# A new hand-written order for the mixer of an encoder layer, with the first step of the second feed-forward layer in it

## The chip, the cores and the metric

The kernel runs on one core of a Trainium2 chip. The metric is the device time of one execution in microseconds (us); lower is better. A core has five engines that each run their own instructions strictly in order and wait for one another through semaphores: PE (TensorE, the matrix products), DVE (VectorE), ACT (ScalarE), POOL (GpSimd) and SP (here only a queue that issues DMAs). The time before is the median of three runs; the profile comes from one more execution.

## The reference, cut to what matters

One encoder layer on 512 positions of width 1024, all in float32: a feed-forward half step, a mixer, a second feed-forward half step and a last norm.

```python
def swiglu(h, w_gate, w_up, w_down):
    return (jax.nn.silu(h @ w_gate) * (h @ w_up)) @ w_down

def reference(x, ...):
    x = x + 0.5 * swiglu(rms_norm(x, ffn1_norm), ffn1_w_gate, ffn1_w_up, ffn1_w_down)
    h = rms_norm(x, mix_norm)
    u = h @ w_in                      # fourier group 512 | q 8x64 | k 2x64 | v 2x64
    f_out = fourier_mixer(u[..., :o0], fnet_w, fnet_b)       # Re(DFT2) per group, then a linear map
    a_out = gqa_attention(u[..., o0:o1], u[..., o1:o2], u[..., o2:], q_norm, k_norm)
    x = x + jnp.concatenate([f_out, a_out], axis=-1) @ w_out
    x = x + 0.5 * swiglu(rms_norm(x, ffn2_norm), ffn2_w_gate, ffn2_w_up, ffn2_w_down)
    return rms_norm(x, final_norm)
```

The feed-forward width is 2752. The attention has 8 query heads of 64 over 2 key heads, with a norm and an axial rotation on q and k.

## The kernel before, in words

The activations lie transposed, as eight tiles of 128 channels x 512 positions (`x[0]` to `x[7]`). Every float32 operand of a product is split into two parts, a rounded high part and the rest, so one product is three matmuls (`product`, L172 to L174): high x high, high x low, low x high. A weight block of 128 x 1024 is loaded by a DMA of the SP queue into one of three raw buffers, its high part is a copy (L865, or L164 in the feed-forward layers) on ACT or DVE, and its low part is raw minus high (`lows`, L131) on DVE or POOL. The splits go into pairs of slots of one ring, and a pair comes free when the last product with the old weights in it has been issued.

The kernel runs in three stages: the first feed-forward layer (0 to 336 us of the profile), the mixer (336 to 492 us) and the second feed-forward layer (492 us to the end). This text is about the mixer and the beginning of the stage behind it.

In the mixer each engine's order is not found by a scheduler. The work is cut into some 620 named operations (`op(...)`), and the string `ORDER` lists their names; the loop `for name in ORDER.split(): ops.pop(name)()` runs inside a block that fixes the order of all five engines as written. The names:

- `wk.r wk.h wk.l`: load of a weight block, its high part, its low part; likewise for `wq0` to `wq3`, `wv`, `f0` to `f3`, `fw`, and `o0` to `o7` of the output projection.
- `q2.5`: the sixth of the eight products of that projection (three matmuls on PE). `q2.sw`, `q2.sd`, `q2.rc`, `q2.rs`: rotation; `.sw` is on ACT, `.sd` are four small DMAs of the SP queue, `.rs` on DVE needs them. `.al` and `.bl` are low parts of the rotated q on DVE.
- `s102 m102 e102 x102 h102 l102`: one attention tile, 128 queries of one head against all 512 keys: scores (two matmuls on PE), scale and row minimum (DVE, L1227), exponential (ACT), 32 x 32 transposes (DVE, L1245), high part (ACT, or DVE if named in `HI_DVE`), low part (DVE, or POOL if named in `LOWS_POOL`). There are 32 tiles; the middle digit is the key head.
- `p0` to `p3`: 128 small matmuls each, probabilities x values of eight tiles. `o00.c o00.a` and so on take the result out (ACT, DVE), `z0.*` and `r0.*` scale it and split it.
- `f..`, `map.`, `d..`, `c..`: the Fourier branch.
- `y5.0` to `y5.7`: the eight products of output block 5; then `y5.x` adds them to `x[5]` (DVE, L1328), `y5.h` and `y5.l` are the two parts of the scaled input of the next layer (ACT, L199; DVE, L203), `y5.q` the square (ACT), `y5.a` its sum over blocks (`acc`, DVE, L1341).

PSUM has eight banks in the mixer (`mix0` to `mix7`), handed out in the order of the string: a product can also wait for the last reader of the bank that it is given.

The second layer opens with the gate block `gate(0, ...)` and the up block `gate(1, ...)`, eight products each. `gate` loads and splits its own weights, then walks k from 0 to 7; the dictionary `between` puts work ahead of a given k. Before the change, `column` (four small matmuls L231 that sum `acc` over the channels; DVE L238 and POOL L245 then make the inverse root) stands ahead of the last product of gate block 0, and `row` (four transposes, L250) ahead of product 3 of gate block 1:

```python
ffn(n2, n3, ..., GROUPS2, lambda gate, column, row: [[gate(0, {KD - 1: column}), gate(1, {3: row})]], Ending)
```

There PE and SP keep the order as written, and a scheduler places the work of DVE, ACT and POOL.

Of the kernel before, what the change touches and what calls it, by code (L numbers as in the profile page):

```python
# [56 lines left out]
k.sw q0.1 k.rc q0.2 q0.3 wq1.l n1.p wv.l q0.4 k.s0 k.s1 q0.5 f2.r q0.6 q0.7 q0.rc q1.0 k.s2 q0.sw q1.1 v.0 kw q1.2
q0.sq kp k.rs q1.3 q0.rs wq2.r q0.ah km k0.0 v.1 k0.2 wq2.h wq2.l q1.4 q1.5 q1.6 q1.7 q1.sw q0.bh v.2 v.3 q0.al k0.3
q0.pq v.4 wq3.r q2.0 q0.bl k1.0 v.5 k1.1 q1.sd v.6 q0.s0 q1.sq v.7 k0.1 q2.1 wq3.h q0.s1 q1.rc vt q1.pq q1.rs k1.3
s002 s003 q1.s0 q0.s2 f0.r f0.h s000 vp m003 wq3.l vm q2.2 m000 e003 q2.3 s001 x003 m002 f0.l m001 f1.r q1.s1 q2.4  # L60
q1.ah q2.5 q3.0 q2.6 q2.7 v0.h q1.al q1.bh h003 q3.1 e002 v0.l e000 x000 q2.sw q2.sq s103 q1.bl vr0.1 q3.2 s100 q3.3
f1.h q3.4 v1.h q3.5 q2.rc q1.s2 s102 s101 m103 x002 q3.6 l003 vr0.2 e103 m100 f1.l v1.l h000 q3.7 q2.sd q2.pq e001
e100 vr0.3 f00.0 q3.sw q2.rs f01.0 q3.sq m101 q3.pq x001 q2.s0 m102 l000 x100 h002 q2.s1 e101 q2.ah q2.al s200 f03.0
q3.sd x101 f3.r k1.2 f02.0 h001 q3.s0 q3.rc s202 q3.rs l002 f00.1 o5.r h100 f2.h q2.s2 q3.ah f3.h vr0.0 s203 q3.al
f2.l f02.1 q3.s1 x103 m203 e102 m202 l001 h101 s300 f00.u q2.bh e203 s201 f01.1 h103 x102 l101 f01.u q3.s2 h102 l103
l100 s302 f3.l f03.1 m200 m300 e202 q3.bh m302 f03.e f11.0 f02.e x203 l102 e302 f11.1 f02.h e200 x202 f03.h q3.bl
m201 fw.r f02.l fw.h e300 x200 p0 f11.u x300 s011 q2.bl e201 o2.r o00.c s303 s301 h203 h202 fw.l o01.c m011 z0.r
f10.0 pos o00.a m303 h200 o01.a h300 f10.1 m301 s012 s112 l203 l202 x201 e303 l200 o1.r s113 s110 h201 x303 m113
e301 f12.0 m112 f13.0 e113 l300 l201 x302 f03.l h303 e112 h302 m012 map1 l303 x301 f10.u f13.1 z1.r x112 map1.h
f12.1 map1.l h301 o2.h f13.e x113 e012 e011 l302 f13.h map0 f12.e f12.h m110 x012 map0.h o1.h l301 p1 f13.l f12.l  # L70
e110 s013 d00 o10.c d01 o11.c map0.l o2.l o1.l h112 x110 m013 vr1.1 d10 d01.h o10.a d00.h o11.a d01.l h012 d00.l d11
vr1.0 d10.h z0.w l112 s213 e013 d10.l x011 c0.s c0.q m213 h113 s111 s010 m010 d11.h h011 h110 s313 c0.c e010 d21
l012 d20 d11.l m111 m313 c1.c l113 e313 d21.h c0.o c1.s x013 d20.h x010 d31 c0.h c1.q d21.l s312 d20.l c0.l d30 s212
h010 l110 e111 z0.p l011 c1.o x111 c2.s o4.r h013 d30.h c1.h vr1.3 z1.w e213 y2.0 d31.h vr1.2 x313 l013 h111 s311
o0.r c2.q c1.l m312 d30.l l111 r0.m o0.h m212 c2.c e312 z1.p y2.1 d31.l e212 c3.c c3.s c2.o c3.q r1.m x212 c2.h c3.o
l010 r0.h m311 o0.l s310 m310 x312 e311 p2 c3.h c2.l e310 h212 c3.l r0.l y1.0 s211 o3.r x213 l212 h313 h312 m211
l313 z2.r s210 h213 l213 x311 m210 e211 o20.c y1.1 h311 y2.2 l312 y1.2 x211 e210 y1.3 o20.a h211 l311 o21.c x210
y2.3 y0.0 x310 y2.4 h210 z2.w h310 o21.a r1.h l210 l310 r1.l y0.1 y0.2 l211 z2.p z3.r y0.3 z3.w r2.m p3 r2.h y2.5
r2.l o30.c o30.a o31.c y2.6 y1.4 z3.p y1.5 y0.4 y1.6 o31.a r3.m r3.h r3.l y0.5 y2.7 o3.h y0.6 o3.l y1.7 y0.7 y3.0
o4.h o5.h y3.1 y3.2 y3.3 y3.4 o6.r o4.l o5.l y0.x y2.x y2.q y2.h y3.5 y4.0 y4.1 y4.2 y3.6 y3.7 y4.3 y4.4 y4.5 y5.0  # L80
# [1558 lines left out]
```

## Time and profile before

| | us |
|---|---|
| median of three runs | 839.28 (839.19 to 839.60) |
| the profiled execution | 835.62 |
| its span, first to last instruction | 833.8 |
| of it PE busy | 820.3 |
| DVE busy | 600.1 |
| ACT busy | 458.2 |
| POOL busy | 134.2 |

The profiled execution is 3.66 us (0.44%) shorter than the median of the runs. Sums below are made against 835.62, and their difference is then carried over to 839.28.

PE is busy nearly all the time, so what counts is its idle time: 13.5 us in the whole span, of which 6.6 us lie between 335 and 500 us. A row of the timeline gives the start, the duration, the engine, the line, the operation, what is written and what is read, and in brackets how long the engine had been idle and who ended that. Instructions overlap a little at their ends, so the distance from one start to the next is shorter than the duration: 0.60 against 0.68 for an `acc` sum, 1.13 against 1.22 for a weight split.

### The profile page before, as it was taken

What the parts mean: (1) busy time and instruction counts of PE and PEld (TensorE: products, weight loads), DVE (VectorE), ACT (ScalarE), POOL (GpSimd) and SP (SyncE); (2) the same over time, 40 slices, a digit from 0 to 9 for tenths busy, and PEclk for the clock granted to TensorE, in tenths of its full rate; (3) what the DMA queues carried; (4) which work ended last, traced back from release to release, by engine and by line L of the source; (5) the groups of instructions that cost most, each with busy time, mean ns of one, the idle gap of its engine ahead of it and who ended that gap; (6) DMA issues with size and microseconds to landing.
All of it is one profiled execution on the core that took longest, in us unless ns stands there. A gap on an engine that the chain in (4) does not pass through costs nothing.

```text
span 833.8 us, 14442 instructions
## 1 busy us (share of the span) xinstructions
PE 820.3 (98%) x5734; PEld 742.3 (89%) x5734; DVE 600.1 (72%) x938; ACT 458.2 (55%) x793; POOL 134.2 (16%) x140
## 2 busy tenths in 40 slices
PE   9999999999999999999989989999999999999997
PEld 6888998899989998889878878899988998899986
DVE  6987884578656857689998478878755884578562
ACT  7754663266434645477887348546533663366452
POOL 0121000000000000168795300200000000000001
PEclk9999999999999999999999999999999999999999
DMA  7787774467374413335351335877563774566122
GB/s 253 189 189 203 190 197 139 121 164 216 91 187 136 137 53 118 127 89 131 106 101 28 100 91 138 212 166 183 172 189 89 180 206 129 122 170 184 45 80 102
DMA packets 50725, 119.33 MB, mean 143 GB/s; under 512 B 5729, under 2 KB 14561, under 8 KB 50529
## 3 DMA queue, kind: packets, MB, share of 16 engines
q1 hardware_dynamic: 38128, 92.57, 33.7%
q0 software_dynamic: 12256, 25.57, 18.6%
q8 instruction: 45, 0.74, 0.4%
q10 hardware_dynamic: 272, 0.26, 0.1%
q14 instruction: 24, 0.19, 0.1%
HBM read 111.83 MB, written 2.10 MB: 137 GB/s over the span
## 4 chain that ended last, share of the span: by engine, by line
PE 89%; DVE 6%; ACT 2%; issue 1%; DMA 1%; POOL 0%; SPq 0%; POOLq 0%; DVEq 0%; ACTq 0%
PE r L441 23%; PE q L441 11%; PE dn L174 9%; PE dn L173 9%; PE dn L172 9%; PE p L441 6%; PE mix L172 3%; PE gu L172 2%; PE gu L173 2%; PE mix L174 2%; PE mix L173 2%; PE gu L174 2%; PE gu L778 2%; PE mix L1261 1%; DVE mix L1227 1%
## 5 line engine op out<-in xcount | busy, mean ns | idle before, releaser
L441 PE MATMUL r<-rt,ring 128*128 128x256 f32 x1686 | 204.9, 276 | 0.0
L441 PEld LDWEIGHTS r<-rt,ring 128*128 128x128 f32 x1686 | 198.5, 188 | 0.9
L173 PE MATMUL dn<-at,ring 128*128 128x512 f32 x295 | 114.8, 389 | 0.0
L174 PE MATMUL dn<-at,ring 128*128 128x512 f32 x295 | 114.8, 389 | 0.0
L172 PE MATMUL dn<-at,ring 128*128 128x512 f32 x295 | 114.8, 389 | 0.0
L441 PE MATMUL q<-rt,ring 128*128 128x256 f32 x840 | 106.6, 276 | 0.0
L386 ACT CAST ring<-s 128x1024 fp32r<-128x1024 f32 x70 | 73.5, 1050 | 57.8 <-DVE s L406 51.0
L441 PEld LDWEIGHTS q<-rt,ring 128*128 128x128 f32 x840 | 100.4, 188 | 0.0
L593 DVE SCALAR_TENSOR_TENSOR gx<-dn,gx 128x512 f32<-128x512 f32 x61 | 42.1, 691 | 80.8 <-PE dn L174 80.8
L358 POOL DMA_DIRECT2D s<-in_wgu x35 | 30.1, 860 | 428.0 <-DMA s<-in_wgu 143.9
L131 DVE TENSOR_TENSOR ring<-s,ring 128x1024 fp32r<-128x1024 f32 x70 | 85.3, 1219 | 0.6 <-ACT ring L386 0.6
L164 ACT CAST ring<-raw_dn 128x768 fp32r<-128x768 f32 (+2 forms) x48 | 40.8, 853 | 76.0 <-PE dn L173 70.5
L174 PEld LDWEIGHTS dn<-at,ring 128*128 128x128 f32 x295 | 55.4, 188 | 11.5
L173 PEld LDWEIGHTS dn<-at,ring 128*128 128x128 f32 x295 | 55.4, 188 | 11.1
L172 PEld LDWEIGHTS dn<-at,ring 128*128 128x128 f32 x295 | 55.4, 188 | 11.1
L441 PE MATMUL p<-rt,ring 128*128 128x256 f32 x420 | 53.3, 276 | 0.0
L131 DVE TENSOR_TENSOR ring<-raw_dn,ring 128x768 fp32r<-128x768 f32 (+2 forms) x48 | 46.7, 977 | 7.4 <-ACT ring L164 7.4
L441 PEld LDWEIGHTS p<-rt,ring 128*128 128x128 f32 x420 | 50.2, 188 | 0.0
L131 DVE TENSOR_TENSOR ring<-raw_g,ring 128x1024 fp32r<-128x1024 f32 x35 | 42.6, 1217 | 0.0
L131 POOL TENSOR_TENSOR its<-x,its 128x512 fp32r<-128x512 f32 x27 | 37.6, 1418 | 7.8 <-ACT its L1247 6.4
L131 DVE TENSOR_TENSOR at<-u,at 128x512 fp32r<-128x512 f32 x35 | 24.2, 692 | 20.2 <-ACT at L496 20.2
L484 DVE TENSOR_TENSOR u<-g,u 128x512 f32<-128x512 f32 x35 | 24.0, 687 | 19.8 <-ACT u L481 19.8
(331 smaller groups left out, 1552.3 us busy)
## 6 DMA issues: line engine op xcount, KB each, us to landing
s<-in_wgu SPq DMA_DIRECT2D x70, 256.0 KB, 4.1
s<-in_wgu POOLq DMA_DIRECT2D x35, 512.0 KB, 6.0
raw_g<-in_wgu SPq DMA_DIRECT2D x35, 512.0 KB, 4.1
raw_dn<-in_wd SPq DMA_DIRECT2D x44, 384.0 KB, 3.8
raw_u<-in_wgu SPq DMA_DIRECT2D x35, 256.0 KB, 4.3
raw_gu<-in_wgu SPq DMA_DIRECT2D x12, 512.0 KB, 3.6
raw_o<-in_wo SPq DMA_DIRECT2D x8, 512.0 KB, 3.6
raw_dn<-in_wd SPq DMA_DIRECT2D x5, 448.0 KB, 4.3
```

The source lines that it names most:

```text
L131: (by or nc.vector).tensor_tensor(out=lo, in0=src, in1=asf(hi), op=ALU.subtract)
L164: nc.scalar.copy(hi[:, :n, :], raw[:, :n, :])
L172: nc.tensor.matmul(ps, whi, mhi, start=first, stop=False)
L173: nc.tensor.matmul(ps, whi, mlo, start=False, stop=False)
L174: nc.tensor.matmul(ps, wlo, mhi, start=False, stop=last)
L358: nc.gpsimd.dma_start(out=blocks(t), in_=up, accum_op=ALU.add)
L386: nc.scalar.copy(ts[0], src)
L441: nc.tensor.matmul(ps[:, c], a[:, ks], b[:, i, c], start=first and i == 0 and o == 0, stop=i == KH - 1 and o == 2, skip_group_check=not fi ...
L484: nc.vector.tensor_tensor(out=self["u"], in0=self["g"], in1=self["u"], op=ALU.mult)
L593: nc.vector.scalar_tensor_tensor(out=x[d][:, t], in0=ps[:, t], scalar=0.5, in1=x[d][:, t], op0=ALU.mult, op1=ALU.add)
L778: nc.tensor.matmul(pss[c], w[:, k % 2, c], m[k], start=k == 0 and m is hh and w is hi, stop=k == KD - 1 and w is lo,)
L1227: nc.vector.tensor_scalar(out=sps[n], in0=sps[n], scalar1=f, scalar2=None, op0=ALU.mult, op1=ALU.min, accum_out=mx)
```

## The change

Four things change. First, the string `ORDER` is a new one: the same operations, in another order on all five engines (from the first projection on), and three more. Second, these three, `g0.r`, `g0.h` and `g0.l`, load and split the weights of the second layer's gate block 0 inside the mixer; `ffn` takes them as `prepared`, and `opening2` issues the loads and splits of block 1 and of the block `2 * NF` (the remainder of the width, used for gate and up) ahead of the products. Third, `column` moves from ahead of product 7 of gate block 0 to ahead of product 0 of gate block 1, one block of products later, and `row` from product 3 to product 6 of gate block 1. Fourth, some splits change engine: the low parts of tile `302` and of the weights `wq3` and `o4` go from POOL to DVE and that of `o7` from DVE to POOL; the high parts of `003`, `wv` and `o5` go from DVE to ACT and those of `wq1` and `o7` from ACT to DVE.

```diff
@@ -36,8 +36,8 @@
 LOWS_POOL = """
-000 001 003 010 011 012 013 100 101 102 103 110 111 113 200 201 202 203 211 212 213 300 301 302 303 311 312 f0 fw o0
-o1 o2 o4 o5 o6 wq3
+000 001 003 010 011 012 013 100 101 102 103 110 111 113 200 201 202 203 211 212 213 300 301 303 311 312 f0 fw o0 o1
+o2 o5 o6 o7
...
 HI_DVE = """
-003 203 o3 o5 o6 wq2 wv
+203 o3 o6 o7 wq1 wq2
...
 ORDER = """
-wk.r wq0.r wv.r cos wk.h wk.l wq0.h k.0 k.1 k.2 k.3 k.4 wv.h k.5 wq0.l k.6 wq1.r k.7 k.sq q0.0 wq1.h n1.c k.pq n1.m
...
+wk.r wq0.r wv.r cos wk.h wk.l wq0.h k.0 k.1 k.2 k.3 k.4 wv.h k.5 wq0.l k.6 wq1.r k.7 k.sq q0.0 wq1.h n1.c q0.1 wq3.r
...
@@ -279,8 +279,16 @@
+            prepared = prepared or {}
+            n_ready = 2 * len(prepared)
+
+            def prepare(c, by_dma=False):
+                prepared[c] = weights(wgu[c], f"gu{n_}_{c}", by_dma=by_dma)
+
             def gate(c, between={}, by_dma=False):
-                whi, wlo = weights(wgu[c], f"gu{n_}_{c}", by_dma=by_dma)
+                if c not in prepared:
+                    prepare(c, by_dma)
+                whi, wlo = prepared.pop(c)
...
@@ -613,9 +621,10 @@
-                    plain.extend(lent)
+                    at_ = len(plain) - n_ready
+                    plain[at_:at_] = lent[n_ready:]
...
@@ -1364,6 +1373,7 @@
+        weight_ops("g0", A["wgu2"][0])
...
+    def opening2(gate, column, row, prepare):
+        with in_full_order():
+            prepare(1)
+            prepare(2 * NF)
+        return [[gate(0, {}), gate(1, {0: column, 6: row})]]
...
-        ffn(n2, n3, A["wgu2"], A["wd2"], A["wdt2"], GROUPS2, lambda gate, column, row: [[gate(0, {KD - 1: column}), gate(1, {3: row})]], Ending)
+        ffn(n2, n3, A["wgu2"], A["wd2"], A["wdt2"], GROUPS2, opening2, Ending, {0: ws["g0"]})
```

What stands where, at three places of which the prediction speaks.

PE at the opening of the second layer, before: the sum of squares (L231) stands between product 6 and product 7 of gate block 0 (`gu2_0`).

```order
L174 MATMUL gu2_0_5408<-ring_61 128x512
L231 MATMUL ss2_0_5430<-ones_82,acc2_5266 128x2 x4
L172 MATMUL gu2_0_5408<-ring_61 128x512
L173 MATMUL gu2_0_5408<-ring_61 128x512
L174 MATMUL gu2_0_5408<-ring_61 128x512
L172 MATMUL gu2_1_5444<-ring_61 128x512
```

PE at the same place in the changed kernel:

```order
L172 MATMUL gu2_0_5419<-ring_61 128x512
L173 MATMUL gu2_0_5419<-ring_61 128x512
L174 MATMUL gu2_0_5419<-ring_61 128x512
L231 MATMUL ss2_0_5445<-ones_82,acc2_5277 128x2 x4
L172 MATMUL gu2_1_5444<-ring_61 128x512
```

The last product of gate block 0 is now ahead of the sum, so PE reaches the sum three matmuls later.

DVE at the end of the mixer, before: `y7.x` (L1328 from `mix1`), `y6.l`, then the two splits of the next weights (`raw_gu2_1` and `raw_gu2_42`, the latter the remainder), `y7.l`, and the last two sums, on which the sum on PE waits.

```order
L203 SCALAR_TENSOR_TENSOR ring_61<-gx_69,ring_61 128x512 x2
L1341 TENSOR_TENSOR acc2_5266<-acc2_5266,sq2_4_0_5344 128x512
L203 SCALAR_TENSOR_TENSOR ring_61<-gx_69,ring_61 128x512
L1328 TENSOR_TENSOR gx_69<-mix1_3403,gx_69 128x512
L203 SCALAR_TENSOR_TENSOR ring_61<-gx_69,ring_61 128x512
L131 TENSOR_TENSOR ring_61<-raw_gu2_1_5440,ring_61 128x1024
L131 TENSOR_TENSOR at2_5401<-raw_gu2_42_5475,at2_5401 128x1024
L203 SCALAR_TENSOR_TENSOR ring_61<-gx_69,ring_61 128x512
L1341 TENSOR_TENSOR acc2_5266<-acc2_5266,sq2_6_0_5380 128x512
L1341 TENSOR_TENSOR acc2_5266<-acc2_5266,sq2_7_0_5378 128x512
```

DVE at the same place in the changed kernel, from `y5.x` (L1337 from `mix1`) on:

```order
L1337 TENSOR_TENSOR gx_69<-mix1_3403,gx_69 128x512
L203 SCALAR_TENSOR_TENSOR ring_61<-gx_69,ring_61 128x512
L131 TENSOR_TENSOR ring_61<-raw_g0_5254,ring_61 128x1024
L203 SCALAR_TENSOR_TENSOR ring_61<-gx_69,ring_61 128x512
L1350 TENSOR_TENSOR acc2_5277<-acc2_5277,sq2_4_0_5328 128x512
L203 SCALAR_TENSOR_TENSOR ring_61<-gx_69,ring_61 128x512
L1337 TENSOR_TENSOR gx_69<-mix4_3406,gx_69 128x512
L203 SCALAR_TENSOR_TENSOR ring_61<-gx_69,ring_61 128x512
L1350 TENSOR_TENSOR acc2_5277<-acc2_5277,sq2_5_0_5366 128x512
L131 TENSOR_TENSOR ring_61<-raw_gu2_1_5410,ring_61 128x1024
L131 TENSOR_TENSOR at2_5405<-raw_gu2_42_5414,at2_5405 128x1024
L203 SCALAR_TENSOR_TENSOR ring_61<-gx_69,ring_61 128x512
```

Behind these stand the last two sums, of `y7` and of `y6`. The two splits of the next weights still stand ahead of `y7.l` and of both sums; what moved is the sum of `y5` (now behind `y7.x`), and six operations stand between `y5.x` and `y7.x`, among them the split `g0.l`.

DVE at the first attention tile, before: `m003` (L1227), the values `vm` (L1036), the next tiles.

```order
L131 TENSOR_TENSOR ks11_3414<-rot_k_3508,ks10_3413 64x512
L953 TENSOR_TENSOR mix0_3402<-mix0_3402,rr_3439 128x8
L954 TENSOR_SCALAR sc2_3436<-mix0_3402 128x8
L1227 TENSOR_SCALAR mix1_3403,mx003_3669<-mix1_3403,sc1_3435 128x512
L1036 TENSOR_TENSOR vm_3672<-mix7_3409,r1_91 128x512
L1227 TENSOR_SCALAR mix6_3408,mx000_3677<-mix6_3408,sc1_3435 128x512
L1245 STREAM_TRANSPOSE x003_3686<-e003_3679 128x512
```

DVE at the same place in the changed kernel:

```order
L131 TENSOR_TENSOR more_3400<-raw_wq3_3498,more_3400 128x1024
L1236 TENSOR_SCALAR mix3_3405,mx003_3664<-mix3_3405,sc1_3435 128x512
L962 TENSOR_TENSOR mix7_3409<-mix7_3409,rr_3439 128x8
L963 TENSOR_SCALAR sc2_3436<-mix7_3409 128x8
L1236 TENSOR_SCALAR mix1_3403,mx000_3671<-mix1_3403,sc1_3435 128x512
L1236 TENSOR_SCALAR mix0_3402,mx002_3687<-mix0_3402,sc1_3435 128x512
L1045 TENSOR_TENSOR vm_3689<-mix6_3408,r1_91 128x512
L1254 STREAM_TRANSPOSE x003_3693<-e003_3678 128x512
```

The split of `wq3` now stands here, ahead of `m003`, and `vm` behind `m000` and `m002`; on PE the transposes `vp` that `vm` reads stand three products later than before (behind `q2.2`, `q3.0` and `q2.3`).

More of the change, by code (lines that the diff above doesn't have):

```diff
@@ L55 @@
 ORDER = """
-wk.r wq0.r wv.r cos wk.h wk.l wq0.h k.0 k.1 k.2 k.3 k.4 wv.h k.5 wq0.l k.6 wq1.r k.7 k.sq q0.0 wq1.h n1.c k.pq n1.m
[L57 to L80, printed above, removed]
@@ new lines @@
+l000 q3.7 q2.pq q2.rs vr0.2 q3.sw f03.0 m103 e101 x001 q3.sq q2.s0 q3.rc vr0.3 f00.0 q2.ah f00.1 q3.pq f02.0 e103
+q2.al l003 m102 q3.sd x101 q3.rs h001 q3.ah f01.0 f2.h q3.s0 s202 s203 f00.u q2.bh e102 q2.s1 s200 x100 vr0.0 f3.h
+s201 h101 l002 q3.al q2.s2 q3.s1 q3.s2 f2.l x102 m203 s302 f01.1 m202 l001 e203 x103 l101 h103 f3.l h102 m200 e202
+f03.1 fw.r l103 f01.u s300 m300 h100 q3.bh f02.1 l102 m302 f03.e l100 f02.e f11.0 x203 f11.1 o2.r e302 f02.h q3.bl
+e200 f11.u x202 fw.h p0 f02.l x200 e300 m201 e201 x300 q2.bl s011 s303 h203 o00.c m011 h202 m303 o01.c h200 o00.a
@@ new lines @@
+fw.l o01.a pos o1.r l203 h300 e303 f03.h s301 x201 l202 f10.0 l200 f10.1 x302 m301 s113 o5.r l300 m113 s112 f10.u
+x303 h201 s012 e301 m112 e113 f13.0 map1 f03.l h303 h302 x301 m012 f12.0 e112 l302 map1.h l201 f13.1 map1.l x112
+h301 l303 o2.h e012 f13.e e011 map0 l301 f12.1 s110 x012 f12.e map0.h f13.h f12.h o1.h m110 e110 p1 f13.l f12.l s013
+z0.r d00 z0.w o10.c o11.c z1.r h112 d00.h o2.l x113 d01 x110 map0.l m013 d01.h o10.a o11.a d00.l d01.l d10 o1.l h012
+s213 d10.h l112 d11 e013 d10.l m213 h113 s313 x011 s010 h110 c0.s d11.h c0.q h011 s111 vr1.0 m010 vr1.1 d21 l012
@@ L753, in encoder, with opening1 @@
     fb = cp.tile([P, 4], F32, name="fb")
-    def opening1(gate, column, row):
+    def opening1(gate, column, row, prepare):
         pss = [bank(f"gu0_{c}") for c in range(4)]
```

24 lines of the change are left out of this document (19 added, 5 removed).

## The prediction

> **What bounds the kernel now.** I began with the page's busy shares, then took the mixer in stretches (the view of windows), then the waits of PE, and last the timeline at the waits that count.
>
> ```profile
> PE 820.3 (98%) x5734; PEld 742.3 (89%) x5734; DVE 600.1 (72%) x938; ACT 458.2 (55%) x793; POOL 134.2 (16%) x140
> ```
>
> PE is the bound of the whole, so the change can only win from PE's idle time, as it adds no matmul and takes none away. Where that idle time lies is told by the stretches. Each row gives the length, then the busy time of PE, weight load, DVE, ACT and POOL.
>
> ```profile
> 364.00:380.00 16.00, 16.00 (x86) 13.68 (x85) 14.20 (x29) 12.49 (x25) 14.82 (x18) 1.00 0.50 103
> 380.00:400.00 20.00, 18.98 (x217) 18.26 (x220) 19.65 (x41) 14.71 (x30) 14.71 (x15) 1.00 0.45 117
> 400.00:420.00 20.00, 19.25 (x269) 17.25 (x263) 19.85 (x46) 16.08 (x42) 16.66 (x14) 1.00 0.33 112
> 420.00:440.00 20.00, 17.87 (x123) 15.16 (x127) 19.50 (x51) 17.88 (x49) 20.00 (x25) 1.00 0.55 94
> 440.00:453.00 13.00, 13.00 (x170) 10.92 (x163) 12.94 (x34) 11.01 (x29) 8.35 (x6) 1.00 0.16 44
> 453.00:492.00 39.00, 39.00 (x284) 32.85 (x284) 20.03 (x36) 14.10 (x27) 7.26 (x3) 1.00 0.22 68
> ```
>
> Between 380 and 440 PE stands idle for 1.02 + 0.75 + 2.13 = 3.90 us, and there DVE is at 19.5 us and more of 20: the attention is bound by DVE. From 453 to 492 PE is full and DVE half empty. What PE waited for:
>
> ```profile
> PE ss L231 <- DVE acc L1341: 2.5, 1, 2.5
> PE mix L172 <- ACT e L1236: 1.1, 2, 0.6
> PE mix L1221 <- DVE qa L131: 1.0, 1, 1.0
> PE mix L1221 <- ACT e L1236: 0.7, 1, 0.7
> PE mix L1221 <- DVE oo L1281: 0.6, 1, 0.6
> PE mix L172 <- ACT fq L1190: 0.3, 1, 0.3
> ```
>
> The largest is the sum of squares at the stage's end; the others, on ACT's `e` too, come while DVE works without a pause. The last tie between the two engines inside the mixer is `p3`, which starts as DVE's `l310` (the second of this pair) ends:
>
> ```profile
> 451.58 1.29 DVE L131 TENSOR_TENSOR its<-x,its 128x512 fp32r<-128x512 f32 x2
> 452.82 1.45 PE L1261 MATMUL mix<-its,vrep 32*128 32x256 f32 x36
> ```
>
> The end of `l310` is 452.87. Behind it PE has no gap up to gate block 0. So there are two terms: when DVE reaches `l310`, and how PE gets from there past the sum of squares.
>
> **Term 1, the path to `l310`.** DVE is not all work in these stretches. Four of its subtractions and sums with two inputs took more than twice their normal time:
>
> ```profile
> 377.71 1.65 DVE L936 TENSOR_TENSOR rot_q<-rot_q,sw_q 128x512 f32<-128x512 f32 x1
> 385.90 0.68 DVE L131 TENSOR_TENSOR its<-x,its 128x512 fp32r<-128x512 f32 x1
> 386.67 2.00 DVE L131 TENSOR_TENSOR qa<-rot_q,qa 64x512 fp32r<-64x512 f32 x1
> 399.82 1.79 DVE L131 TENSOR_TENSOR el<-fe,eh 128x512 fp32r<-128x512 f32 x1
> 423.81 1.63 DVE L131 TENSOR_TENSOR its<-x,its 128x512 fp32r<-128x512 f32 x1
> 386.84 1.28 POOL L131 TENSOR_TENSOR its<-x,its 128x512 fp32r<-128x512 f32 x1
> 399.78 1.29 POOL L131 TENSOR_TENSOR ring<-raw_fw,ring 128x512 fp32r<-128x512 f32 x1 [2.52 <-ACT ring L865]
> 422.85 2.71 POOL L1053 DMA_DIRECT2D vrep<-vst  x5
> 388.85 2.23 POOL L131 TENSOR_TENSOR its<-x,its 128x512 fp32r<-128x512 f32 x1 [0.72 <-ACT its L1247]
> ```
>
> The second row is the undisturbed price, 0.68. Against it the others lost 0.97, 1.32, 1.11 and 0.95 us, together 4.35, and 3.38 of it from 385 us on. Beside two of them POOL ran a subtraction of its own, and beside `l112` (423.81) it issued the DMAs of `vrep`. In the last row it went the other way round: POOL took 2.23 instead of 1.28 beside a weight split on DVE. These are the only places where DVE's price departs so far, so I read a resource that only one of the two has at a time. [...]
>
> Up to `x100` (385.98 before) the pieces of the new order are these.
>
> ```profile
> 364.89 0.76 DVE L1227 TENSOR_SCALAR_CACHE_REDUCE mix<-mix,sc 128x512 f32<-128x512 f32 x1 [0.78 <-PE mix L1222]
> 373.43 0.76 DVE L1227 TENSOR_SCALAR_CACHE_REDUCE mix<-mix,sc 128x512 f32<-128x512 f32 x1 [0.74 <-POOL sc L963]
> 495.16 1.22 DVE L131 TENSOR_TENSOR ring<-raw_gu,ring 128x1024 fp32r<-128x1024 f32 x1
> 496.29 1.22 DVE L131 TENSOR_TENSOR at<-raw_gu,at 128x1024 fp32r<-128x1024 f32 x1
> 370.93 0.69 ACT early L907
> 373.48 3.38 DMA sw_q<-early
> L131 POOL TENSOR_TENSOR more<-raw_wq,more 128x1024 fp32r<-128x1024 f32 x1 | 2.5, 2532 | 0.4 <-ACT more L865 0.4
> ```
>
> The split of `wq3`, 1.13 on DVE by the distance of the two split rows (POOL took 2.53 for it), fills the 0.78 us of waiting ahead of `m003` and costs 0.35. `vm` waits for the transposes `vp`, three products of 3 x 0.227 later than before: 0.9 us of waiting, where nothing else stands in front. The 0.74 us at 373.43 go, and so do the 0.97 us that `q2.rs` was blocked, since the `vrep` issues now stand behind it. The swap of q takes 5.9 us from its copy on ACT (370.93) to its landing (376.86): with `q2.sw` where the order has it, `q2.rs` waits 0.5 and `q3.rs` 1.05. The high part of `003` leaves DVE, 0.34. Sum: 0.35 + 0.9 + 0.5 + 1.05 − 0.74 − 0.97 − 0.34 = 0.75 slower; `m003` starts 0.6 earlier since `vp` and the second scores stand behind it on PE, and two short waits of 0.45 together before `m003` go. Net about 0.3 us earlier. Bounds: both swaps free, 1.85 earlier; each 1.5 us later still, 2.7 later.
>
> From there to the end of `l310` it was 452.87 − 385.98 = 66.9 us, of which 3.38 blocked and about 0.45 idle (the rows at 400, 420 and 440 lack 0.15, 0.50 and 0.06 of full, and I leave a quarter of a microsecond of it to the seams between instructions). The same DVE operations come in the new order, and the low part of `302` more, 0.6. With nothing blocked and half of the idle time left, `l310` ends 0.3 + 3.38 + 0.23 − 0.6 = 3.3 us earlier. PE can follow that: its 3.90 us of idle time ahead of `p3` is more.
>
> But the new order has meetings of its own. On POOL and DVE these pairs stand side by side: `l001` and the split of `f2`; `fw.l` and `f02.l`; `303` and `f03.l`; `l301` and `l302`; the `vrep` issues and `l112`. [...] A loss was 1.1 us in the mean of the four rows. Half of five is 2.5 x 1.1 = 2.75 us. I take that, since before the same kind of meeting cost DVE four times and nothing in the new order keeps the engines apart. Bounds: none, and all five at the full length of a POOL instruction, 5 x 1.29 = 6.45. Term 1 is thus 3.3 − 2.75 = 0.5 us earlier, from 3.3 earlier to 3.2 later.
>
> **Term 2, the end of the stage.**
>
> ```profile
> 492.26 0.39 PE L172 MATMUL gu<-ring 128*128 128x512 f32 x1
> 499.65 1.02 PE L231 MATMUL ss<-ones,acc 128*128 128x2 f32 x8 [2.46 <-DVE acc L1341]
> 500.53 0.49 PE L172 MATMUL gu<-ring 128*128 128x512 f32 x1
> 501.33 0.40 PE L172 MATMUL gu<-ring 128*128 128x512 f32 x1
> 493.90 0.69 DVE L1328 TENSOR_TENSOR gx<-mix,gx 128x512 f32<-128x512 f32 x1
> 494.50 0.74 DVE L203 SCALAR_TENSOR_TENSOR ring<-gx,ring 128x512 fp32r<-128x512 f32 x1
> 497.43 0.75 DVE L203 SCALAR_TENSOR_TENSOR ring<-gx,ring 128x512 fp32r<-128x512 f32 x1
> 498.09 1.41 DVE L1341 TENSOR_TENSOR acc<-acc,sq 128x512 f32<-128x512 f32 x2
> 492.49 0.39 PE L173 MATMUL gu<-ring 128*128 128x512 f32 x1
> ```
>
> Call G the first matmul of gate block 0 (492.26). Before, the first of block 1 is at 501.33, G + 9.07; 24 matmuls at 0.23 from start to start (492.26 to 492.49) and the sum's 0.88 make 6.4, and the rest is the wait. Moving `column` behind product 7 lets PE do 0.68 us of work during that wait and removes nothing else: DVE must end the sums earlier or the wait only shrinks by this. It does. In the new order `y5.x` follows `y5.7` at G − 3.9 (six products ahead of G), 0.60 (493.90 to 494.50), then `y1.l` 0.66 (494.50 to 495.16), `g0.l` 1.13, `y5.l` 0.66, a sum 0.60, `y4.l` 0.66, so `y7.x` starts at G + 0.4, against 493.90 = G + 1.64 before. `y7.x` 0.60, `y6.l` 0.66, the sum of `y5` 0.60, two splits 2.26, `y7.l` 0.66 and the last two sums 1.41 end at G + 6.6. PE is there at G + 5.5 and waits about 1.2; `ss` starts 0.15 behind the sums as before, at G + 6.8, and block 1 at G + 7.65. The gain is 9.07 − 7.65 = 1.4 us. The moved `row` sets when DVE and POOL have the inverse root: it was wanted by product 3 of block 1 and is now wanted by product 6, three products (2.0 us) later for a sum 1.4 + 0.7 later relative to the weights; I cost that at nothing, its cover being those 2 us. Bounds: only the 0.68 of cover, if `y7.x` comes no earlier; all of the wait, 2.46.
>
> Loads of block 0 (`g0.r`) now go out some 20 us ahead, from a queue that has 0.22 of DMA share in that stretch: nothing. The highs that change engine are on ACT, at most 17.88 of 20 us: nothing, unless DVE gets faster; then ACT's `e` is late next. `o4.l` on DVE (1.13) and `o7.l` on POOL lie in 453 to 492, where DVE has 19 us to spare.
>
> **Sum.** 0.5 + 1.4 = 1.9 us less than 835.62 of the profiled execution, 833.7; carried over to the median, 839.28 − 1.9 = 837.4, or −0.23%. I call within 0.2% (1.68 us) no change.
>
> **The rivals.** [...] (b) DVE is blocked as long as before, 3.38 us or a little more: term 1 vanishes and the tail is left, or is cut to its 0.68; 837.9 to 838.6, so about 838.4, no change. For it: the number of meetings is what it was. [...] (d) The change doesn't do what it says at the end: `y7.l` and the sums still stand behind two splits, so PE still waits; the 1.2 us above is that wait; if it stays whole and the tail gains 0.68 alone, the time is 839.28 − 0.5 − 0.68 = 838.1, inside (b).
>
> **The numbers.** The forecast (two or three meetings lost; its own range 836.2 to 837.6) has 0.36, (a) 0.10, (b) with (d), from 837.6 to 839.9, 0.28, and (c), from five meetings on or from a like loss at the two swaps, 0.26. Faster by over 0.2% holds (a) and the forecast, 0.46; no change is (b), 0.28; slower is (c), 0.26. The range runs from (a) at 834.8 to (c) with five meetings, 841.4 with the swaps 0.4 later than taken.
>
> **What would show it.** PE's wait at `ss` near 1.2 us and block 1 at 7.65 us behind block 0: term 2 right; a wait over 2 says it isn't. `p3` 0.5 us earlier, DVE waits of 0.9 at `vm` and 1.05 at `q3.rs`, and two or three lengthened DVE rows between 385 and 450 us: term 1 right. Wrong would be a `p3` that moves by more than 3 us either way, a wait of PE on ACT's `e` that grows, or PE waiting behind block 1 for the inverse root.

## The result, and the profile after

The changed kernel takes 834.51 us in the median of 20 runs (831.53 to 839.08); the kernel before, run beside it 20 times, 839.11 us (835.35 to 842.33). The ratio is 0.9954, with a 95% interval of 0.9937 to 0.9971: faster by 0.46%, 3.9 us, where 1.9 us were forecast. The profiled execution took 831.53 us, 4.09 us less than that of before; that of the changed kernel is the shortest of its 20 runs, and that of before lies near the short end of its own. Lines of the mixer are 9 higher than before (L1227 is now L1236).

By stage, from the starts of the same instructions in the two traces: the first product of the mixer comes 0.30 us earlier, from there to `p3` it is 2.45 us less (116.92 and 114.47), from `p3` to the first matmul of gate block 0 0.07 less, from there to block 1 1.30 less (9.06 and 7.76), and the rest 0.11 more. So term 1 (the path to `l310`) came out at 2.45 instead of 0.5, and term 2 (the stage's end) at 1.3 as against 1.4.

First the page's busy shares, then the stretches (length, then busy PE, weight load, DVE, ACT, POOL; the third number from the end is the granted clock) and what PE waited for between 335 and 501 us, all of the changed kernel:

```profile
PE 818.9 (99%) x5734; PEld 742.5 (89%) x5734; DVE 602.6 (73%) x939; ACT 458.7 (55%) x794; POOL 131.9 (16%) x138
```

```profile
364.00:380.00 16.00, 16.00 (x89) 13.84 (x89) 14.95 (x32) 13.49 (x28) 13.55 (x18) 1.00 0.64 141
380.00:400.00 20.00, 20.00 (x251) 18.83 (x250) 19.72 (x39) 14.63 (x34) 16.65 (x17) 1.00 0.39 90
400.00:420.00 20.00, 20.00 (x245) 18.76 (x244) 19.58 (x55) 18.44 (x50) 16.77 (x15) 1.00 0.43 141
420.00:440.00 20.00, 16.90 (x191) 14.83 (x192) 20.00 (x48) 16.08 (x40) 17.64 (x20) 1.00 0.51 78
```

```profile
PE mix L172 <- DVE ring L131: 1.6, 1, 1.6
PE mix L173 <- DVE ring L131: 0.8, 1, 0.8
PE ss L231 <- DVE acc L1350: 0.8, 1, 0.8
PE mix L172 <- ACT e L1245: 0.4, 1, 0.4
```

PE's idle time fell from 13.5 to 10.8 us in the whole span, 2.7 of the 4.1 us; the other 1.4 went out of its busy time, which the prediction had taken as fixed. DVE is as full as before and still sets the pace of the attention; PE now stands idle in one stretch only, 3.10 us between 420 and 440, 2.46 of it in front of products of the Fourier branch (`c3.s`, `c2.s`), and the waits at the scores of tiles 200 and 012 are gone. The tail, PE and then DVE:

```profile
489.44 0.39 PE L172 MATMUL gu<-ring 128*128 128x512 f32 x1
496.31 1.02 PE L231 MATMUL ss<-ones,acc 128*128 128x2 f32 x8 [0.76 <-DVE acc L1350]
497.20 0.49 PE L172 MATMUL gu<-ring 128*128 128x512 f32 x1
489.89 0.69 DVE L1337 TENSOR_TENSOR gx<-mix,gx 128x512 f32<-128x512 f32 x1
494.02 0.75 DVE L203 SCALAR_TENSOR_TENSOR ring<-gx,ring 128x512 fp32r<-128x512 f32 x1
494.68 1.48 DVE L1350 TENSOR_TENSOR acc<-acc,sq 128x512 f32<-128x512 f32 x2
```

`y7.x` starts 0.45 us behind block 0 (G + 0.4 was said), the sums end at G + 6.7, the sum on PE starts at G + 6.9, and PE's wait shrank from 2.46 to 0.76 us.

The lengthened two-input subtractions and sums of DVE, and the wait at `vm`:

```profile
366.98 0.69 DVE L1045 TENSOR_TENSOR vm<-mix,r 128x512 f32<-128x512 f32 x1 [0.68 <-PE mix L1040]
375.90 1.61 DVE L944 TENSOR_TENSOR sw_q<-sw_q,early 128x512 f32<-128x512 f32 x1
385.33 0.68 DVE L131 TENSOR_TENSOR qa<-rot_q,qa 64x512 fp32r<-64x512 f32 x1
396.74 0.65 DVE L131 TENSOR_TENSOR el<-fe,eh 128x512 fp32r<-128x512 f32 x1
420.46 1.48 DVE L131 TENSOR_TENSOR its<-x,its 128x512 fp32r<-128x512 f32 x1
431.62 1.33 DVE L131 TENSOR_TENSOR el<-fo,eh 128x512 fp32r<-128x512 f32 x1
448.79 1.29 DVE L131 TENSOR_TENSOR its<-x,its 128x512 fp32r<-128x512 f32 x2
```

`q3.al` (385.33) and `f02.l` (396.74), 2.00 and 1.79 us before, are short now. Lost from there on, each beside work of POOL: 0.79 at `l112` and 0.66 at `c1.l` (431.62), 1.45 us, against 3.38 before. `l310` (the second of the last row) ends at 450.08, and `p3` starts at 450.07.

### The profile page after: what moved, and what is told of

Read it like the earlier page. It is cut to its first block, busy times and chain, and to the rows that moved or that the text cites. A ratio compares the mean times of both kernels' runs of the same rounds, so it can differ in the third digit from the quotient of the medians.

```text
span 829.7 us, 14444 instructions
## 1 busy us (share of the span) xinstructions
PE 818.9 (99%) x5734; PEld 742.5 (89%) x5734; DVE 602.6 (73%) x939; ACT 458.7 (55%) x794; POOL 131.9 (16%) x138
## 2 busy tenths in 40 slices
DMA packets 50724, 119.33 MB, mean 144 GB/s; under 512 B 5728, under 2 KB 14560, under 8 KB 50528
## 4 chain that ended last, share of the span: by engine, by line
PE 95%; DVE 3%; issue 1%; POOLq 0%; POOL 0%; ACT 0%; DVEq 0%
PE r L449 23%; PE q L449 11%; PE dn L173 9%; PE dn L172 9%; PE dn L174 9%; PE p L449 6%; PE mix L172 3%; PE mix L174 3%; PE mix L173 3%; PE gu L787 3%; PE gu L172 2%; PE gu L174 2%; PE gu L173 2%; PE mix L1270 2%; PE mix L1101 1%; PE last L1475 1%
```

## The experiments

What they gave, with the kernel before run beside each. Ratio and interval are to that kernel; the other columns come from each run's profiled execution: `p3` behind the first product of the mixer, PE's wait at the sum of squares, block 1 behind block 0. The intervals reach 0.1 to 0.3% to each side, so the time alone doesn't tell apart two rows whose ratios differ by less than about 0.25%.

| run | median us | ratio (95%) | `p3` | wait | block 1 |
|---|---|---|---|---|---|
| the kernel before | 838.4 to 839.8 | 1 | 116.92 | 2.46 | 9.06 |
| the changed kernel | 834.51 | 0.9954 (0.9937 to 0.9971) | 114.47 | 0.76 | 7.76 |
| old order up to `p3` | 836.59 | 0.9972 (0.9958 to 0.9985) | 118.57 | 0.76 | 7.76 |
| old order behind `p3` | 838.34 | 0.9995 (0.9979 to 1.001) | 116.97 | 2.46 | 9.27 |
| `column` back | 835.50 | 0.9968 (0.9950 to 0.9985) | 119.52 | 1.95 | 8.53 |
| sums ahead of splits | 833.39 | 0.9937 (0.9914 to 0.9961) | 114.45 | 0 | 6.25 |
| `wq2.h` later | 833.02 | 0.9930 (0.9914 to 0.9946) | 116.11 | 0.76 | 7.76 |
| before, two meetings out | 837.71 | 0.9988 (0.9977 to 1.000) | 117.27 | 2.46 | 9.61 |
| one meeting in | 835.41 | 0.9958 (0.9945 to 0.9971) | 118.16 | 0.76 | 7.76 |
| `vr1` on SP | 832.63 | 0.9931 (0.9911 to 0.9951) | 113.79 | 0.76 | 7.76 |
| before, tail alone | 839.62 | 0.9993 (0.9976 to 1.001) | 117.60 | 1.06 | 8.42 |
| two lows back on POOL | 838.15 | 0.9979 (0.9959 to 0.9998) | 119.33 | 0.76 | 7.76 |
| three edits together | 830.79 | 0.9898 (0.9871 to 0.9924) | 115.27 | 0 | 6.25 |
| the three, `vr0` on SP too | 834.12 | 0.9955 (0.9936 to 0.9974) | 117.72 | 0 | 6.25 |

### Which part of the order carries the gain

Two kernels take the string `ORDER` apart at `p3`, with the engines of the splits as they belong to each part. The first has the old string up to `p3` and the new one, with the new opening, behind it:

```diff
 ORDER = """
-wk.r wq0.r wv.r cos wk.h wk.l wq0.h k.0 k.1 k.2 k.3 k.4 wv.h k.5 wq0.l k.6 wq1.r k.7 k.sq q0.0 wq1.h n1.c q0.1 wq3.r
+wk.r wq0.r wv.r cos wk.h wk.l wq0.h k.0 k.1 k.2 k.3 k.4 wv.h k.5 wq0.l k.6 wq1.r k.7 k.sq q0.0 wq1.h n1.c k.pq n1.m
...
```

> The old order (and the old engines of the splits) up to p3, the new order, splits and opening behind it. Theory: the two parts add. The old first part brings back the blocked and waiting VectorE, so l310 ends near 452.9 and p3 starts near 452.8, as in the kernel before; the tail keeps its 1.3 us (block 1 at 7.7 to 7.8 us behind block 0). Time 1.3 us below the kernel before, 837.8 by its median of 839.1. Rival: the gain comes from the tail and from the loads and splits that it takes out of the opening, and p3 is only a symptom; then this run is 3.5 to 4.6 us below, like the changed kernel.

The other is the reverse, on the kernel before:

> The new order up to p3, the old order behind it, and the old opening (sum of squares ahead of product 7, no split of block 0 in the mixer). Theory: p3 starts near 450.1 and the tail is the old one, 9.0 to 9.1 us from block 0 to block 1 with a wait of 2.4 us at the sum; time 2.4 to 2.8 us below the kernel before, about 836.5. Rival (the tail alone carries the gain): within 0.5 us of the kernel before, 839.

The tail does what was expected, 7.76 us, and the run with it alone is 2.3 us faster than before (1.3 to 3.5 by its interval). Its `p3` isn't what was expected: 118.57 instead of the 116.92 of the kernel before, in the same order; in this trace PE waited 2.42 us at the scores of tile 200 and ran 3.4 us at half clock. The new first part alone gives nothing that can be told from 0. Its `p3` at 116.97 is not the 114.47 of the changed kernel, though the order up to there is the same. So the expectation of 2.4 us for the first part fell, and the intervals don't tell whether the two parts add up to 3.9. The next runs show what makes the same order longer in one execution than in another.

### The sum of squares put back

```diff
-        return [[gate(0, {}), gate(1, {0: column, 6: row})]]
+        return [[gate(0, {KD - 1: column}), gate(1, {3: row})]]
```

> The changed kernel with the sum of squares back ahead of product 7 of gate block 0 and the row back ahead of product 3 of block 1; order and splits stay new. Theory: the sums on VectorE end 6.6 to 6.7 us behind the first matmul of block 0 as they do now, PE reaches the sum 0.68 us earlier and waits 0.68 us longer, about 1.5 us; block 1 comes at 8.3 to 8.4 us instead of 7.76. Time 0.6 us above the changed kernel. Rival: the move is the whole of the tail's gain (block 1 at 9.1, 1.3 us above).

Block 1 comes at 8.53 instead of 7.76: 0.77 us, close to the 0.68 that one product is worth, so the move alone is 0.77 of term 2's 1.30 us; the rest, 0.53, falls to the earlier `y7.x` by subtraction. This trace also shows how the first part gets longer. DVE, then POOL and PE:

```profile
351.12 0.69 DVE L874 CAST ring<-raw_wq 128x1024 fp32r<-128x1024 f32 x1 [1.47 <-DMA raw_wq<-in_wins]
364.08 3.44 DVE L131 TENSOR_TENSOR more<-raw_wq,more 128x1024 fp32r<-128x1024 f32 x1
363.74 2.69 POOL L131 TENSOR_TENSOR ring<-raw_f,ring 128x1024 fp32r<-128x1024 f32 x1 [1.57 <-ACT ring L874]
367.57 0.80 PE L174 MATMUL mix<-ring,more 128*128 128x512 f32 x1 [1.66 <-DVE more L131]
```

and the same instructions in the changed kernel's own profile:

```profile
349.60 0.70 DVE L874 CAST ring<-raw_wq 128x1024 fp32r<-128x1024 f32 x1 [0.30 <-DMA raw_wq<-in_wins]
362.68 1.22 DVE L131 TENSOR_TENSOR more<-raw_wq,more 128x1024 fp32r<-128x1024 f32 x1
363.40 2.77 POOL L131 TENSOR_TENSOR ring<-raw_f,ring 128x1024 fp32r<-128x1024 f32 x1 [2.62 <-ACT ring L874]
```

The new order has `wq2.h` earlier on DVE than the old one, and there DVE waits for the load of `wq2`. Where the load lands 1.47 us after DVE wants it, instead of 0.30, DVE comes to `wq3.l`, the split that the change put on DVE, 0.3 us behind POOL's split of `f0` instead of 0.7 us ahead of it. It then takes 3.44 us, and PE waits for it. In the run with the old tail it was the same (a wait of 1.45 and again 3.44 us). Of the seven traces with `wq2.h` in its early place, DVE waited 1.33 to 1.47 us there in three, 0.30 in one and not at all in three. The late load isn't all of this trace's length, whose `p3` is 5.05 us behind that of the changed kernel: PE's wait of 1.66 us was followed by 3.4 us at half clock, and the swap of q2 came 0.75 us late.

### That race taken out

`wq2.h` goes back to its old place, ahead of `wq2.l`:

```diff
-q0.sq wq2.h k.s1 q1.1 q0.sw k.s2 kw q0.pq q1.2 kp k.rc k.rs km q0.rs q0.ah wq2.l
+q0.sq k.s1 q1.1 q0.sw k.s2 kw q0.pq q1.2 kp k.rc k.rs km q0.rs q0.ah wq2.h wq2.l
```

> The changed kernel with one operation moved: the high part of wq2 on VectorE stands right ahead of its low part, behind the rotation of q0, as late as in the kernel before. Theory: in the changed kernel VectorE stops there until the load of wq2 has landed (0.30 us in one execution, 1.47 and 1.45 in two others); where it lands late, VectorE comes 1.5 us later to the split of wq3, GpSimd's split of f0 has started by then, VectorE is blocked for 2.2 us and PE waits 1.7 us for the low part. With the move the late landing is covered: no execution has that wait, p3 comes 114.3 to 114.6 us behind the first product of the mixer, and the median falls by 1 to 2 us, to about 833. Rival: the long executions have another cause (the clock by itself); the median stays within 0.5 us of the changed kernel's 834.5 and half of the executions stay above 836.

The median fell to 833.02, and none of its six runs was over 834.87, where 7 of 20 of the changed kernel were over 836.2: the expectation of the time held. Six runs are few: with 7 long ones in 20, six in a row without one would come by chance in one case of 13. The rival, the clock, isn't ruled out either. The seven long runs have a mean clock of 0.994 to 0.997, and eleven of the thirteen others 0.998 or 0.999; the six runs here have 0.998, the longest 0.996. A late load and a stretch at half clock can come together, as in the trace above, and which of the two makes most runs long isn't shown. The expectation of `p3` (114.3 to 114.6) fell in the profiled execution, the longest of the six, at 116.11: `wq3.l` is short, but the next transfer landed late. The swap of q2 came 0.54 us after DVE wanted it, and both products of `q2.rs` then met POOL (1.65 and 1.66 us).

### The meetings themselves

The kernel before with two meetings moved apart, `l001` behind `l101` on POOL and `f02.l` behind `x200` and `x300` on DVE:

```diff
-m202 l001 h101 s300 f00.u q2.bh e203 s201 f01.1 h103 x102 l101
+m202 h101 s300 f00.u q2.bh e203 s201 f01.1 h103 x102 l101 l001
...
-fw.r f02.l fw.h e300 x200 p0 f11.u x300
+fw.r fw.h e300 x200 p0 f11.u x300 f02.l
```

> The kernel before with two operations moved so that VectorE and GpSimd don't meet there: the low part of 001 on GpSimd behind that of 101, and that of f02 on VectorE behind the transposes of 200 and 300. Theory: the two subtractions that took 2.00 and 1.79 us take 0.68, the end of l310 and p3 come 2.0 to 2.4 us earlier, 114.5 to 114.9 us behind the first product of the mixer instead of 116.92, and the time is 2.0 to 2.4 us below the kernel before (836.2 against 838.4 to 839.1). Rival: the blocked time is hidden, or returns at the next meeting; p3 within 0.5 us of 116.9 and no gain.

`q3.al` and `f02.l` take 0.69 and 0.65 us, as expected, and `p1` starts 78.39 us behind the first product instead of 79.94. But `p3` is at 117.27, no earlier than before, and the time falls by 1.0 us instead of 2.0 to 2.4, with an interval that reaches 0: the rival held. One part came back as a new meeting: `c1.l`, 0.65 us before, now takes 1.64 beside POOL. Another went in PE's clock, which was at 0.57 in the four microseconds after PE had waited 0.75 and 0.32 us; behind the same two waits (0.74 and 0.32) it stayed at 1.00 in the profile of the kernel before. DVE and POOL at `c1.l`, and the stretches behind:

```profile
433.64 1.64 DVE L131 TENSOR_TENSOR el<-fo,eh 128x512 fp32r<-128x512 f32 x1
433.44 1.28 POOL L131 TENSOR_TENSOR its<-x,its 128x512 fp32r<-128x512 f32 x1
```

```profile
434.00:436.00 2.00, 1.28 (x5) 0.71 (x5) 2.00 (x4) 2.00 (x6) 1.51 (x2) 1.00 0.21 33
436.00:440.00 4.00, 3.74 (x15) 3.37 (x15) 4.00 (x12) 1.81 (x5) 4.00 (x3) 0.57 0.01 2
```

The reverse, on the changed kernel, puts `f02.l` one transpose later, into POOL's split of `fw`:

```diff
-x202 fw.h p0 f02.l x200 e300 m201
+x202 fw.h p0 x200 f02.l e300 m201
```

> The changed kernel with one meeting put in: the low part of f02 on VectorE stands one transpose later, where GpSimd is in the split of fw. Theory: this subtraction takes 1.7 to 1.9 us instead of 0.65, everything behind it on VectorE is 1.1 us later, and so is p3: 115.5 us behind the first product of the mixer instead of 114.46, the time 1.1 us above the changed kernel. Rival: PE's own waits cover it; p3 moves by less than 0.3 us.

`f02.l` is lengthened by 1.03 us, as expected. The time doesn't tell it from the changed kernel: the ratios differ by 0.04%, with intervals of 0.13% and 0.17% to each side, and its trace has a late swap (0.71 us) and 3.4 us at half clock beside it, `p3` at 118.16 instead of 115.5. Inconclusive on the time.

The change's own edit on this is the moved engine of two low parts. Undone alone:

```diff
 LOWS_POOL = """
+302 wq3
```

> The changed kernel with the low parts of wq3 and of tile 302 back on GpSimd, the rest new. Theory (VectorE is the bound of the attention): VectorE has 1.13 + 0.6 us less to do, the meeting of the split of wq3 with that of f0 can't come, and p3 is up to 1.7 us earlier, time 1 to 2 us below the changed kernel's 834.5. Rival: GpSimd, at 16.7 of 20 us, becomes late with 2.5 + 1.3 us more (p0 waits for its low parts), p3 is 0 to 2 us later.

The rival held, by another way than it said. By the ratios the kernel lost 2.1 us of its 3.9, though DVE has 1.7 us less to do; the two intervals just overlap, but the gain of 1 to 2 us that the theory expects is outside. In the trace `p3` is 4.86 us later: 1.5 lie ahead of `p0`, where the load of `wq2` was late too (1.33 us), and 3.35 between `p1` and `p2`. There and at `q1.rs`, POOL's longer queue meets DVE at three more places. DVE, then POOL:

```profile
364.14 2.75 DVE L945 TENSOR_TENSOR rot_q<-rot_q,sw_q 128x512 f32<-128x512 f32 x1
416.88 4.72 DVE L131 TENSOR_TENSOR el<-fe,eh 128x512 fp32r<-128x512 f32 x2
363.59 2.75 POOL L131 TENSOR_TENSOR more<-raw_wq,more 128x1024 fp32r<-128x1024 f32 x1 [0.75 <-ACT more L874]
415.86 2.39 POOL L131 TENSOR_TENSOR more<-raw_o,more 128x1024 fp32r<-128x1024 f32 x1
418.22 2.82 POOL L131 TENSOR_TENSOR ring<-raw_o,ring 128x1024 fp32r<-128x1024 f32 x1
```

2.75 instead of 0.69 at `q1.rs`, 4.72 instead of 1.3 at `f13.l` and `f12.l` beside two whole weight splits: this is a loss of the kind that the slower rival (c) counts, 3.4 us at one place, in a kernel one step away.

### The tail

```diff
+LATER = "y7.l y7.a y6.a".split()
...
             for name in ORDER.split():
-                ops.pop(name)()
+                if name not in LATER:
+                    ops.pop(name)()
...
         with in_full_order():
+            for name in LATER:
+                ops.pop(name)()
             prepare(1)
             prepare(2 * NF)
```

> The changed kernel, with the low part of y7 and the last two sums put ahead of the two weight splits on VectorE (they are now issued just ahead of the loads of block 1). Theory: the wait at the sum (0.76 us) and the one at product 7 (0.24 us) are made by the two splits (2.26 us); without them the sums end 4.3 us behind the first matmul of block 0, PE waits for nothing there, block 1 comes at 6.4 us, 1.0 to 1.4 us earlier, if the splits (now ending at 6.6) and the inverse root stay hidden. Rival: the split of block 1 is then late, PE waits for it at the second matmul of block 1, and 0.3 us or less is won.

Block 1 comes at 6.25 and PE waits for nothing there; the split of block 1 isn't late. The run is 1.4 us better than the changed kernel by the ratios (0.9937 and 0.9954), as expected, but the intervals overlap: that the wait and 1.51 us from block 0 to block 1 are gone is shown by the trace. PE at the sum and the first matmul of block 1:

```profile
495.32 0.95 PE L232 MATMUL ss<-ones,acc 128*128 128x2 f32 x8
496.12 0.49 PE L173 MATMUL gu<-ring 128*128 128x512 f32 x1
```

The same with the old order of the mixer (and block 0 loaded and split in the opening):

> The old order and engines of the mixer, nothing of block 0 split in it, and the tail alone changed: the sum of squares behind product 7, and the low part of y7 and the last two sums ahead of the two splits on VectorE. Theory: the sums end about 5.0 us behind the first matmul of block 0, PE (there at 5.5) doesn't wait, block 1 comes at 6.3 us instead of 9.06: 2.8 us. As a wait of 1.7 to 2.5 us of PE is followed by 3.4 us at half clock in some executions (1.7 us), the mean gain is up to 1 us more: time 2.8 to 3.8 us below the kernel before, 835 to 836. Rival (no such tie of wait and clock): exactly 2.8, and a mean clock that stays as it was (0.995).

It gave nothing, and its trace says where the gain went, into a new wait on ACT:

```profile
496.18 1.05 ACT L305 CAST at<-rawt 128x1024 fp32r<-128x1024 f32 x1 [1.25 <-DMA rawt<-in_wdt]
497.14 0.72 ACT L199 ACTIVATE ring<-gx 128x512 fp32r<-128x512 f32 x1
```

The scheduler set a weight copy, whose load had not landed, ahead of the high part of `y7`; DVE waited 1.96 us for this, and block 1 came at 8.42. So this run doesn't test the tie of waits and clock that it was meant for.

### The DMAs that POOL issues

`l112` (the row at 420.46) and the first product of `q2.rs` (375.90) took 1.48 and 1.61 us, instead of 0.68, while POOL issued DMAs of the values (417.87 to 421.65 and 373.46 to 377.80). First those of the second head (`vr1`) go to SP's queue (with their operands read as plain float32); the question is whether `l112` then takes 0.7 us or stays at 1.4 or more:

```diff
-                    nc.gpsimd.dma_start(
+                    (nc.sync if v == 1 else nc.gpsimd).dma_start(
```

> The changed kernel with the sixteen DMAs of the second value head issued from SP's queue, not from GpSimd's. [...] By the price of the row p3 is 0.8 us earlier; if SP's queue delays the values instead, p2 is later.

`l112` is long still, but POOL, freed, is now in a low part of its own there, so this decides nothing (DVE, then POOL):

```profile
421.47 1.47 DVE L131 TENSOR_TENSOR its<-x,its 128x512 fp32r<-128x512 f32 x1
421.10 1.29 POOL L131 TENSOR_TENSOR its<-x,its 128x512 fp32r<-128x512 f32 x1 [2.75 <-ACT its L1256]
```

Elsewhere the meeting at `c1.l` is gone, `p3` is 0.68 us earlier, and the run is 1.9 us below the changed kernel by the ratios, with intervals that overlap.

The best version joins this with the two edits above (`wq2.h` later, sums ahead of the splits):

> Three edits on the changed kernel together: the high part of wq2 later, the low part of y7 and the last sums ahead of the two splits, the DMAs of the second value head from SP's queue. Theory: they act at different places and add: 1.5 us from the tail, 0.7 us from the meeting of c1 that goes, 1 to 1.5 us in the median from the executions with the late landing; 830 to 831 in the median, 829.5 in the best execution. Rival: the gains overlap (each frees the same waits); 832.5, no better than each of them alone.

The median is 830.79 us, 0.9898 of the kernel before. The three gains, taken one by one from the ratios, would give 0.9890: within the interval they add. It beats both kernels, clear of both intervals.

Last, the first head's DMAs (`vr0`) too, behind the swaps in SP's queue. The question is whether the first product of `q2.rs`, without POOL's issues beside it, takes 0.7 us, with `p3` at 113.4 to 114.4 instead of 115.3, or stays at 1.5 us or more:

> The three edits of the run before, and the DMAs of the first value head from SP's queue too, behind the swaps of q2 and q3; GpSimd issues no value DMAs any more. [...] The time follows p3, 829 to 830, or stays at 830.8; if the values come late by SP's queue, p0 is later than 61.1 us behind the first product.

The first product of `q2.rs` takes 0.68 us in this one trace, and 1.17 to 1.73 in all other traces of the new order, where POOL issued such DMAs. But `p0` pays for it. It starts at 59.44, ahead of the 61.1 that was said, and stops in the middle: SP issues the values until 391 us, POOL waits for their landing, and PE for POOL, and 3.4 us at half clock follow. `p3` is at 117.72 instead of 113.4 to 114.4, and the run is 4.8 us above the one before it.

```profile
377.23 0.68 DVE L944 TENSOR_TENSOR sw_q<-sw_q,early 128x512 f32<-128x512 f32 x1
394.21 4.20 POOL L131 TENSOR_TENSOR its<-x,its 128x512 fp32r<-128x512 f32 x3 [3.74 <-DMA vrep<-its]
398.46 3.81 PE L1270 MATMUL mix<-its,vrep 32*128 32x256 f32 x68 [2.33 <-POOL its L131]
```

## Why the prediction was right, and where its size was off

The way was right, and by the ratio the time lies in the range (835.4 us, 0.9954 of the 839.28 on record). The forecast of 1.9 us was half of what came. The time is below the forecast's own 836.2 to 837.6 and nearer to rival (a), that no meeting costs DVE anything (839.28 − 3.3 − 1.4 = 834.6), which had a chance of 0.10; yet this isn't what came, as DVE lost 1.45 us. (By this sum the range would start at 834.6, not at 834.8; nothing hangs on it here.) The other end, 841.4, is that 834.6 with all five meetings lost at 1.29 us each, 6.45, and 0.4 for the swaps. No run shows five such losses; the changed kernel lost at two places.

- **Term 2** held in each step: `y7.x` at G + 0.45 for 0.4, block 1 at 7.76 for 7.65, the wait 0.76 for 1.2 (0.24 us of waiting at product 7, which the prediction didn't have, is part of the difference). The part on `column` alone (0.68 of cover) was 0.77 in the run that undoes it. `row` at product 6 cost nothing: PE has no wait in the second layer's opening behind the sum.
- **Term 1** was mis-sized, 2.45 for 0.5, in three of its pieces. The meetings ("half of five is 2.75") cost 1.45: of the five named pairs only `l112` was lost by DVE, and one not named, `c1.l`. That DVE loses at half of its meetings was an estimate that no run shows; over the fourteen traces 42 of 165 operations beside a subtraction of POOL were lengthened by over 0.25 us. The swaps ("`q2.rs` waits 0.5 and `q3.rs` 1.05") cost nothing in the profiled execution, 1.55 less than said. Against these two, the 0.97 us that `q2.rs` was blocked did not go, because POOL still issued the `vrep` DMAs beside it (373.46 to 377.80), not behind it as the prediction had it; it lost 0.92 on its other product. 0.5 + 1.3 + 1.55 − 0.9 = 2.45. That this closes to the hundredth is luck: the wait at `vm`, 0.68 for 0.9, isn't in it. The waits at 364.89 and 373.43 went as said.
- What the prediction didn't see is that these pieces aren't fixed numbers. In the run with the old tail DVE waited 1.45 us for the load of `wq2` instead of 0.30, `wq3.l` took 3.44 us instead of 1.22, and the new order was 2.5 us longer in the mixer (116.97 and 114.47). With the order and the engines unchanged, `p3` came at 114.45, 114.47, 116.97 and 119.52 in the new first part and at 116.92, 117.60 and 118.57 in the old one; so the 2.45 us are those of two favourable executions, and that they came near the measured gain is in part luck. The 0.5 us for the swap, absent in the profile, is there in four other traces of the new order (0.54 twice, 0.71, 0.75). It took each wait on a DMA as the one trace had it.
- The slower rival (c), losses of DVE beyond those of the forecast, was seen one step away: with two low parts back on POOL, `f13.l` and `f12.l` lost 3.4 us beside two whole weight splits (2.39 and 2.82 us on POOL). The changed engine of `wq3.l` and `302.l`, which the prediction counted only as 1.13 and 0.6 us more work for DVE, is what keeps the changed kernel clear of it, worth 2.1 us by the ratios, with intervals that just overlap.
- What the two halves of the order are worth apart stays open in part: old first part with new tail −2.3 us, new first part with old tail −0.4, both −3.9, with intervals of 1.1 to 1.4 us to each side. That the late landing of `wq2` cost the new first part its gain is shown in two traces; how often it comes in the kernel's own 20 runs is argued from their spread and from the three late loads in seven traces.

## What to carry to other kernels

Over the fourteen traces of this case 42 of 165 two-input operations of DVE beside a subtraction of POOL were lengthened by over 0.25 us. Where two engines lengthen each other's instructions like that, count the places where they come at the same time, and move work off the one whose queue makes more of them, even to the busier engine: two low parts back on POOL cost 2.1 us by the ratios, with intervals that just overlap. A wait on a load in the middle of an in-order engine can change what meets what behind it from one execution to the next: at `wq2.h` it was 0.30 us in one trace and 1.47 in another, in which `wq3.l` took 3.44 us instead of 1.22. Put first uses of a load where their engine comes late anyway. And of work that stands together at the end of a stage, that for which the next engine waits goes first: with `y7.l` and the last sums ahead of the splits PE's wait of 0.76 us was gone.

## What the runs showed of the hardware that was not expected

**PE at half clock after short waits.** The profiles of the two kernels have no such stretch ahead of their last 4 us, but nine of the twelve other traces do. In the run with `wq2.h` later PE waited 0.24 and 0.76 us at 496.6 and 498.1, and then:

```profile
496.00:498.00 2.00, 1.10 (x4) 0.30 (x2) 1.85 (x3) 0.86 (x1) 0.00 (x0) 1.00 0.92 307
498.00:500.00 2.00, 1.90 (x11) 1.76 (x12) 1.46 (x3) 1.74 (x4) 0.21 (x1) 0.81 0.45 182
500.00:501.00 1.00, 1.00 (x3) 0.77 (x3) 0.33 (x1) 0.64 (x1) 0.83 (x1) 0.50 0.56 49
501.00:502.00 1.00, 1.00 (x4) 0.77 (x3) 0.90 (x1) 0.00 (x0) 0.00 (x0) 0.50 0.62 238
502.00:503.00 1.00, 1.00 (x5) 0.81 (x4) 0.00 (x0) 0.00 (x0) 0.00 (x0) 0.68 0.71 254
503.00:504.00 1.00, 1.00 (x6) 0.83 (x5) 0.00 (x0) 0.00 (x0) 0.00 (x0) 1.00 0.69 168
```

The clock is 0.50 for about 3.4 us, and the stage behind is 1.6 us longer (334.11 from block 1 to the end, 332.53 in the changed kernel). At the sum of squares a wait of 1.95 or 2.46 us was followed by it in three of four traces, one of 0.76 to 1.06 us in two of seven, and no wait in none of three. It also came within the mixer behind waits of 1.15, 1.66, 2.02, 2.33 and 2.42 us and behind the pair of 0.75 and 0.32, and not behind seven others of 1.63 to 1.89 us. So on these few traces a wait of PE was followed by such a stretch in some executions and not in others. What that is worth to the change isn't measured apart. One such stretch takes 0.002 off the mean clock of 835 us. The median of the mean clock is 0.998 in the 20 runs of the changed kernel and 0.994 in 78 runs of the kernel before that were made beside the experiments, so fewer such stretches can be a good part of the 3.9 us. On the other hand, the runs with 0.998 or more are 4.2 us apart in the median too (833.77 for 11 of the changed kernel, 837.98 for 7 of the kernel before).

**DVE beside POOL, counted.** Over the fourteen traces, no two-input SBUF operation of DVE in the mixer ahead of `p3` was lengthened by over 0.25 us where POOL ran nothing or only its small 128x8 operations (437 of them). Beside a subtraction of POOL 42 of 165 were, beside DMA issues of POOL 13 of 105. The last run shows, in one trace, that the lengthening at `q2.rs` goes with the issues. Why 13 of the 105 were lengthened and the others not is open.
